# Last feed-forward of a decoder layer: chunks 6 to 17 of gate and up with tokens on the output's partitions

## The chip, the cores and the metric

The kernel runs on one core of a Trainium2 chip. The metric is device time of one execution in microseconds (us). The kernel before takes 858.42 us, the median of three runs (857.91 to 858.55).

## The reference

One layer, on 512 tokens of width 1024, all in float32: a feed-forward at half weight, a mixer (gated linear recurrence beside sliding-window attention), and a second feed-forward at half weight, each with a norm before and after.

```python
def swiglu(x, w_gu, w_down):
    gate, up = jnp.split(x @ w_gu, 2, axis=-1)
    return (jax.nn.silu(gate) * up) @ w_down

for l in range(DEPTH):                 # DEPTH = 1
    x = x + 0.5 * rms_norm(swiglu(rms_norm(x, ffn1_pre_g[l]), ffn1_w_gu[l], ffn1_w_down[l]), ffn1_post_g[l])
    y = hybrid_mixer(rms_norm(x, mix_pre_g[l]), ...)
    x = x + rms_norm(y, mix_post_g[l])
    x = x + 0.5 * rms_norm(swiglu(rms_norm(x, ffn2_pre_g[l]), ffn2_w_gu[l], ffn2_w_down[l]), ffn2_post_g[l])
```

The hidden width is 2816: 22 chunks of 128 for gate and as many for up.

## The kernel before

Every float32 product is made of three matrix multiplies on rounded parts: each operand is split into a high part (a cast on ACT, `whi_…` for weights, `hh…` for hidden values) and a low part (a subtraction on DVE, `wlo_…`, `hl…`), and high×high, high×low and low×high are added up in PSUM.

Gate and up of neighbouring chunks are the four blocks of a 2×2 block product, which is done with 7 block products instead of 8. It exists in two shapes.

- A **quad** (`Hidden.quad`, matmuls on L858) makes 2 chunks. Weights are stationary and 256 tokens move in each matmul; the output has hidden columns on its partitions. 168 matmuls.
- An **octo** (`Hidden.octo`, matmuls on L933) makes 4 chunks. Blocks of the input stay, and 512 weight columns move in each matmul; the output has tokens on its partitions. 168 matmuls as well. The down product wants hidden columns on the partitions, so the result is turned: DVE transposes 32×32 squares (L943), SP stores the 4 chunks to HBM in four transfers (`h_… <- z…`, L947), and they are fetched again (`hx… <- h_…`, L993 or L1006). The squares leave the tokens in a *dealt* order, 32 by 32 from the two halves, and the sums of the input blocks must be dealt too (L618 rather than L620).

The down product of 4 chunks also has two shapes: `seven_down`, 7 block products of the hidden values (84 matmuls of 512 columns, L1833 to L1835 in the last feed-forward), which needs sums of hidden blocks, each split into high and low; and a classical one, 24 matmuls of 512 columns for each chunk (L1809 to L1811). Results of a group are added into an array in HBM by accumulating transfers on POOL's queue (L1081).

The first feed-forward makes chunks 0 to 3 by plain products and chunks 4 to 19 by four octos, the second to fourth each followed by the `seven_down` of the group before it, so that an octo's hidden values have time for the way through HBM; chunks 20 and 21 come from a quad, beside which the fetched chunks 16 to 19 are split, and a classical down product of six chunks ends it. The last feed-forward (hidden tiles named `…b`) goes by `GROUPS2`, (0,6), (6,10), (10,14), (14,18), (18,22): chunks 0 to 5 by plain products and a classical down product; each of the next three groups by two quads and a `seven_down`; the last group by two quads and a last product, token block by token block (`ybl`, L1809 to L1811 again), followed by the norm, the residual (L1901 to L1921) and the output.

Weights come in units, handled by `Weights`, one list in the order of use. SP loads raw tiles (5 buffers); `take` hands out one unit and prepares those up to four ahead: for some units a combination of two blocks on DVE (`pre`, lines L292, `raw <- raw, raw`), the cast on ACT (L281), the subtraction on DVE (L285). `W.later(n, …)` defers work until n more units have been taken; `beside` hooks run between block products. Nothing else sets the order: each engine runs its instructions in the order in which the program lists them.

In the last group the hidden values of a quad come out in two halves, `u2` and `g1`: the first half of the tokens and the second. They are split on L871 (ACT) and L874 (DVE).

Of the kernel before, what the change touches and what calls it, by code (L numbers as in the profile page):

```python
# [8 lines left out]
F32 = mybir.dt.float32  # L9
# [8 lines left out]
NB = T // P  # L18
# [15 lines left out]
SEVEN_DOWN1, SEVEN_DOWN2 = (4, 16), (6, 18)  # L34
# [15 lines left out]
class Weights:  # L50
# [13 lines left out]
    def unit(self, raw, cast, low, pre=None):  # L64

        self.units.append((raw, cast, low, pre))
        self.left[raw] += 1
# [10 lines left out]
    def round(self):  # L78
        if self.rounded < len(self.units):
            raw, cast, _, pre = self.units[self.rounded]  # L80
# [39 lines left out]
def tile_layer(ctx: ExitStack, tc: tile.TileContext, out: bass.AP, **ins: bass.AP):  # L120
# [144 lines left out]
    def add_octo(w_gu, f, name):  # L265
# [12 lines left out]
        def unit(block, n, pre=None):  # L278
# [8 lines left out]
            W.unit(block[0], cast, low, pre)  # L287
# [101 lines left out]
    for f0, f1 in GROUPS2:  # L389
        for f in range(f0, f1, 2):  # L390
            (add_gate_up if f < CLASSIC2 else add_quad)(w2, f, "b")
        if SEVEN_DOWN2[0] <= f0 < SEVEN_DOWN2[1]:
            add_seven_down(ins["ffn2_w_down"], f0, "b")
        elif f1 < FC:
            for dh in range(2):
                for f in range(f0, f1, 4):
                    add_down(f, min(4, f1 - f), dh)
        else:
            for f in range(f0, f1, 4):
                for dh in range(2):  # L400
                    add_down(f, min(4, f1 - f), dh)
# [161 lines left out]
    class Next:  # L563
# [37 lines left out]
        def sums(self, k):  # L601
# [174 lines left out]
    class Hidden:  # L776
# [68 lines left out]
        def quad(self, f, last, ahead, seven_down=False, beside=lambda i: None):  # L845
# [3 lines left out]
            hs = None if seven_down else [(t2k(f"hh{n}{j}", F32R), t2k(f"hl{n}{j}", F32R)) for j in range(2)]  # L849
# [31 lines left out]
            u2, g1 = ((t2k if seven_down else wt)(f"{s}{n}") for s in ("u2", "g1"))  # L881
            seven(A, "b11", True)
            act.copy(B, A)
            seven(D, "t3", True)
# [18 lines left out]
            act.activation(g1, A, AF.Silu)  # L903
            if last:
# [1045 lines left out]
```

## Time and profile before

| what | value |
|---|---|
| median of three runs | 858.42 us |
| the profiled execution | 857.46 us, of which the span from first to last instruction 855.8 us |
| PE (matmuls) | 846.8 us, 99% of the span, 5252 instructions |
| DVE | 712.2 us, 83% |
| ACT | 520.3 us, 61% |
| POOL | 210.8 us, 25% |
| granted TensorE clock | 0.999 |

Times are microseconds from the start of the span. PE is TensorE, DVE VectorE, ACT ScalarE, POOL GpSimd, SP SyncE, whose queue starts most transfers. A busy engine need not be the one that sets the end; for that one reads what an engine waited for, and the chain of work that ended last. Rows of a group read: line, engine, operation, output<-inputs, count, duration. In stages by window, each engine has its busy time and, in brackets, its instructions; PEclk is the granted clock and the DMA share is the mean over 16 DMA engines. The durations that matmul rows show overlap each other; what one matmul costs is a run's length over its count.

### The profile page before, as it was taken

To read this page: it belongs to the slowest core of one execution; us is meant where nothing else is said; L and a number is where in the kernel's file an instruction comes from. 1 tells how busy PE (TensorE), PEld (TensorE's weight loads), DVE (VectorE), ACT (ScalarE), POOL (GpSimd) and SP (SyncE) were. 2 spreads that over 40 slices of the span, in tenths; PEclk is the share of its full clock that TensorE was granted. 3 is DMA by queue.
4 is the path that set the end of the run, shared out by engine and by line. 5 is a ranking of instruction groups with operands and counts; after the bars stand their busy time and mean duration, and the time that the engine had idled before them with its cause. 6 is when DMAs were issued, how large, how long until landed. Compare 5 with 4: busy or idle time off the path is not lost.

```text
span 855.8 us, 13837 instructions
## 1 busy us (share of the span) xinstructions
PE 846.8 (99%) x5252; PEld 762.6 (89%) x5252; DVE 712.2 (83%) x1008; ACT 520.3 (61%) x871; POOL 210.8 (25%) x228
## 2 busy tenths in 40 slices
PE   9999999999999999999999999999999999999996
PEld 9988788988988999988888899888998998998995
DVE  5988999979889865989888589788788789888856
ACT  6645746666575754648788346444566657658552
POOL 2022000230320424426453155211101303204402
PEclk9999999999999999999999999999999999999999
DMA  7249329397694999133301230356833946938912
GB/s 248 75 149 341 127 64 324 83 253 235 149 262 144 195 281 311 51 99 97 101 2 50 68 130 1 86 161 215 277 100 107 228 134 154 216 99 199 292 52 98
DMA packets 118914, 133.85 MB, mean 156 GB/s; under 512 B 23152, under 2 KB 85952, under 8 KB 118336
## 3 DMA queue, kind: packets, MB, share of 16 engines
q1 hardware_dynamic: 103504, 98.23, 36.2%
q0 software_dynamic: 15200, 34.61, 18.1%
q8 instruction: 41, 0.67, 0.3%
q14 instruction: 25, 0.20, 0.1%
q10 hardware_dynamic: 144, 0.13, 0.0%
HBM read 96.25 MB, written 36.70 MB: 155 GB/s over the span
## 4 chain that ended last, share of the span: by engine, by line
PE 87%; DVE 6%; ACT 3%; POOL 1%; DMA 1%; issue 1%; SPq 0%; DVEq 0%; ACTq 0%; POOLq 0%
PE ab L858 11%; PE aa L933 10%; PE db L858 5%; PE da L933 4%; PE yaa L1309 3%; PE bb L858 3%; PE ba L933 3%; PE yda L1309 2%; PE aa L858 1%; PE yb L1811 1%; PE yb L1810 1%; PE yb L1809 1%; PE wo L1764 1%; PE yea L1309 1%; PE yba L1309 1%
## 5 line engine op out<-in xcount | busy, mean ns | idle before, releaser
L1081 POOL DMA_DIRECT2D yp_a<-stage x42 | 36.4, 1084 | 179.8 <-ACT stage L1078 169.8
L1081 POOL DMA_DIRECT2D yp_b<-stage x42 | 36.8, 1139 | 148.3 <-ACT stage L1078 143.2
L479 PE MATMUL ya<-hha,whi_ad 128*128 128x512 f32 x62 | 24.1, 389 | 0.0
L481 PE MATMUL ya<-hha,wlo_ad 128*128 128x512 f32 x62 | 24.1, 389 | 0.0
L480 PE MATMUL ya<-hla,whi_ad 128*128 128x512 f32 x62 | 24.1, 389 | 0.0
L665 POOL TENSOR_TENSOR acca_r<-acca_r,sq_r 128x512 f32<-128x512 f32 x6 | 8.0, 1328 | 45.4 <-ACT sq_r L510 45.4
L1809 PE MATMUL yb<-whi_bd,hhb 128*128 128x512 f32 x48 | 18.7, 389 | 0.0
L1810 PE MATMUL yb<-wlo_bd,hhb 128*128 128x512 f32 x48 | 18.7, 389 | 0.0
L1811 PE MATMUL yb<-whi_bd,hlb 128*128 128x512 f32 x48 | 18.7, 389 | 0.0
L211 DVE TENSOR_TENSOR wlo_bd<-raw_bd,whi_bd 128x1024 fp32r<-128x1024 f32 x10 | 12.1, 1214 | 5.3 <-ACT whi_bd L206 5.3
L498 PE MATMUL an<-xh_mx,whi_xl 128*128 128x256 f32 x64 | 15.8, 287 | 0.0
L792 POOL TENSOR_TENSOR usb<-usb,gsb 128x512 f32<-128x512 f32 x5 | 7.2, 1443 | 34.1 <-DVE usb L789 22.8
L499 PE MATMUL an<-xh_mx,wlo_xl 128*128 128x256 f32 x64 | 15.5, 283 | 0.0
L1909 POOL TENSOR_TENSOR yp_b<-yp_b,grow 128x512 f32<-128x512 f32 x6 | 7.7, 1291 | 27.2 <-ACT ysq L1902 27.2
L479 PE MATMUL gt<-xh_mx,whi_gt 128*128 128x512 f32 x32 | 14.2, 444 | 0.0
L480 PEld LDWEIGHTS ya<-hla,whi_ad 128*128 128x128 f32 x62 | 11.6, 188 | 2.4
L479 PEld LDWEIGHTS ya<-hha,whi_ad 128*128 128x128 f32 x62 | 11.6, 188 | 2.4
L481 PEld LDWEIGHTS ya<-hha,wlo_ad 128*128 128x128 f32 x62 | 11.6, 188 | 2.4
L1810 PE MATMUL ybl<-wlo_bd,hhb 128*128 128x512 f32 (+1 forms) x36 | 13.2, 366 | 0.0
L1809 PE MATMUL ybl<-whi_bd,hhb 128*128 128x512 f32 (+1 forms) x36 | 13.2, 366 | 0.0
L1811 PE MATMUL ybl<-whi_bd,hlb 128*128 128x512 f32 (+1 forms) x36 | 13.2, 365 | 0.0
L1857 POOL DMA_DIRECT2D yp_b<-stage x8 | 4.4, 550 | 35.4 <-ACT stage L1856 35.0
(2157 smaller groups left out, 3723.5 us busy)
## 6 DMA issues: line engine op xcount, KB each, us to landing
yp_a<-stage POOLq DMA_DIRECT2D x50, 256.0 KB, 8.9
yp_b<-stage POOLq DMA_DIRECT2D x50, 256.0 KB, 7.5
h_a<-za SPq DMA_DIRECT2D x16, 256.0 KB, 4.2
hxa<-h_a SPq DMA_DIRECT2D x16, 256.0 KB, 18.4
raw_bd<-in_ffn_w_down SPq DMA_DIRECT2D x4, 1024.0 KB, 5.8
xn<-in_x SPq DMA_DIRECT2D x8, 256.0 KB, 4.2
xT_hbm<-xT POOLq DMA_DIRECT2D x2, 1024.0 KB, 9.4
yp_a<-yp_a SPq DMA_DIRECT2D x8, 256.0 KB
```

The costliest lines, as they stand in the source:

```text
L479: pe.matmul(ps, hi[:, k, :], xh, start=start, stop=False)
L480: pe.matmul(ps, hi[:, k, :], xl, start=False, stop=False)
L481: pe.matmul(ps, lo[:, k, :], xh, start=False, stop=stop)
L498: pe.matmul(ps[:, sl], hi[:, k, :], xh, start=k == 0, stop=False)
L499: pe.matmul(ps[:, sl], lo[:, k, :], xh, start=False, stop=False)
L858: pe.matmul(o, w[:, k, js], x, start=first and i + j + k == 0, stop=k == 3 and i == 2, skip_group_check=True)
L933: pe.matmul(b[tb], x[:, blk], w[:, k, :], start=first and q + k + j == 0, stop=q + k == 2 and j == 2, skip_group_check=True)
L1081: pool.dma_start(o, st.rearrange("p (a b) -> p a b", a=2) if len(o.shape) == 3 else st, accum_op=ALU.add)
L1309: pe.matmul(o, a[:, k, ms], x[:, js], start=first and i + k + m % 2 == 0, stop=k == 1 and i == 2, skip_group_check=True)
L1809: pe.matmul(ps, hh[:, blk], hi[:, k, cs], start=start, stop=False)
L1810: pe.matmul(ps, hh[:, blk], lo[:, k, cs], start=False, stop=False)
L1811: pe.matmul(ps, hl_[:, blk], hi[:, k, cs], start=False, stop=stop)
```

## The change

- Chunks 6 to 9, 10 to 13 and 14 to 17 of the last feed-forward are made by one octo each instead of two quads. Their hidden values go through HBM.
- The order becomes: octo(6), octo(10), `seven_down`(6), octo(14), `seven_down`(10), quad(18), the down product of chunks 14 to 17, quad(20), the last product. The down product of chunks 14 to 17 is classical; its four chunks are fetched into free tiles and split beside quad(18).
- The input sums of the last feed-forward are dealt, for the quads as well. So a block of 128 tokens of chunks 18 to 21 has columns from both `u2` and `g1`.
- In octo units, of the first feed-forward too, `fill` issues the combination and the cast of the next unit before the subtraction of the current one (`first`).
- In `seven_forms_of`, again for both feed-forwards, the hidden values that came back are split one half or one whole block product earlier: the first at 2.5 rather than 3.5, the second at 3.5 rather than 4.5, the third at 4.5 rather than 5.
- Some tiles are taken from other places (`spare`, `room`, `tiles`), and the load that was deferred to the first quad is now issued inside the classical down product of chunks 0 to 5.

```diff
@@ -88,7 +88,9 @@
         while self.split < min(self.taken + n, len(self.units)):
             if self.rounded == self.split:
                 self.round()
-            raw, _, low, _ = self.units[self.split]
+            if early and self.rounded == self.split + 1 < len(self.units) and self.units[self.rounded][4]:
+                self.round()
+            raw, _, low, _, _ = self.units[self.split]
             low(self.tiles[raw], *self.ready[self.split])
             self.split += 1
             self.left[raw] -= 1
@@ -284,7 +286,7 @@
             def low(raw, hi, lo):
                 dve.tensor_sub(lo, of(block), hi.bitcast(F32))
 
-            W.unit(block[0], cast, low, pre)
+            W.unit(block[0], cast, low, pre, True)
@@ -386,19 +388,23 @@
         for i in range(0, n, 2):
             add_unit(r, lambda raw, i=i: raw[:, i:i + 2, :], 2, T, f"bd{f + i}{dh}")
 
-    for f0, f1 in GROUPS2:
-        for f in range(f0, f1, 2):
-            (add_gate_up if f < CLASSIC2 else add_quad)(w2, f, "b")
-        if SEVEN_DOWN2[0] <= f0 < SEVEN_DOWN2[1]:
-            add_seven_down(ins["ffn2_w_down"], f0, "b")
-        elif f1 < FC:
+    for g, (f0, f1) in enumerate(GROUPS2):
+        if g == 0:
+            for f in range(f0, f1, 2):
+                (add_gate_up if f < CLASSIC2 else add_quad)(w2, f, "b")
             for dh in range(2):
                 for f in range(f0, f1, 4):
                     add_down(f, min(4, f1 - f), dh)
-        else:
-            for f in range(f0, f1, 4):
-                for dh in range(2):
-                    add_down(f, min(4, f1 - f), dh)
+            continue
+        (add_octo if f1 < FC else add_quad)(w2, f0, "b")
+        if f1 == FC:
+            for dh in range(2):
+                add_down(GROUPS2[g - 1][0], 4, dh)
+        elif g > 1:
+            add_seven_down(ins["ffn2_w_down"], GROUPS2[g - 1][0], "b")
+    add_quad(w2, f0 + 2, "b")
+    for dh in range(2):
+        add_down(f0, f1 - f0, dh)
@@ -603,11 +609,8 @@
 
             n = f"{self.name}{k}"
             xa, xb, t13, t24 = (wt(f"{s}_{n}") for s in ("xa", "xb", "ta", "tb"))
-            some = (lambda nm, dt: spare.pop() if spare else t2k(nm, dt)) if self.name != "a" else t2k
-            if self.name != "a" and k < 2:
-                spare.extend(fours(f"sums{k}", F32R))
-            b11 = some(f"b11_{n}", F32R)
-            highs = [some(f"{s}h_{n}", F32R) for s in ("b2", "t13", "t24")]
+            b11 = t2k(f"b11_{n}", F32R)
@@ -793,7 +796,7 @@
 
         def split(self, f):
             us, n = self.u.pop(f), f"{self.name}{f}"
-            hh, hl = t2k(f"hh{n}", F32R), t2k(f"hl{n}", F32R)
+            hh, hl = (spare.pop(), spare.pop()) if spare else (t2k(f"hh{n}", F32R), t2k(f"hl{n}", F32R))
             act.copy(hh, us)
             dve.tensor_sub(hl, us, hh.bitcast(F32))
             self.hs[f] = (hh, hl)
 
             def low_parts(x, h):
-                if seven_down:
-                    (self.seven_right if h else self.seven_left)(f, x, last)
-                    return
                 def own(t):
                     return dealt(t)[:, 2 * h:2 * h + 2] if self.nxt.dealt else t[:, HALF[h]]
@@ -996,13 +997,14 @@
                 self.forms, self.blocks = {}, {}
                 self.seven_left(f, x[0, 0], 0)
 
-            return {1: [fetch], 3.5: [begin], 4.5: [lambda: self.seven_right(f, x[0, 1], 0)], 5: [lambda: self.seven_left(f, x[1, 0], 1)],
-                    5.5: [lambda: self.seven_right(f, x[1, 1], 1)], 6: [lambda: self.steps.pop(0)()]}
-
-        def fetched(self, f, h_hbm):
+            first, second = ([lambda: self.seven_right(f, x[0, 1], 0)], [lambda: self.seven_left(f, x[1, 0], 1)]), [lambda: self.seven_right(f, x[1, 1], 1)]
+            step = [lambda: self.steps.pop(0)()]
+            return {1: [fetch], 2.5: [begin], 3.5: first[0], 4.5: first[1], 5.5: second, 6: step}
@@ -1797,7 +1786,7 @@
             W.fill(3)
     late = [(c, W.take(0)) for c in range(EARLY, KD)]
 
-    n2 = Next("f2", "ffn2_pre_g")
+    n2 = Next("f2", "ffn2_pre_g", dealt=True)
@@ -1834,34 +1823,57 @@
                 pe.matmul(banks[i], hh[:, js], lo[:, k, :], start=False, stop=False, skip_group_check=True)
                 pe.matmul(banks[i], hl_[:, js], hi[:, k, :], start=False, stop=k == 1, skip_group_check=True)
 
-    for g, (f0, f1) in enumerate(GROUPS2[:-1]):
-        if g:
-            if g == 1:
-                W.later(4, W.load, 2)
-            seven_down(hid, f0, by_tokens, lambda half, dh, i: parts[2 * half + i, dh])
-            continue
-        turns = [(turn_back, c) for c in range(KD)]
-        hs = hid.classic(f1, banks, {2.5: turns[:2], 3: turns[2:4], 3.5: [(n2.sums, 0)], 4: [(n2.lows, 0)] + turns[4:6], 4.5: [(n2.sums, 1)], 5: [(n2.lows, 1)] + turns[6:]}, AHEAD - 1)
+    def classic_down(hs, f0, f1, others=lambda dh, f: None, **kw):
         for dh in range(2):
-            ybanks = [bank(f"yb{g}{dh}{tb}") for tb in range(NB)]
                 if f % 2 == 0:
                     w = W.take()
                 for tb in range(NB):
                     mm3_out(ybanks[tb], hs[f - f0], tb, w, f % 2, ALL, f == f0, f == f1 - 1)
-                if g == 0 and (dh, f) in ((0, 0), (0, 2), (1, 2), (1, 4)):
-                    (n2.sums if f == 2 * dh else n2.lows)(2 + dh)
+                others(dh, f)
             for tb in range(NB):
                 st = t2k("stage")
                 act.activation(st, ybanks[tb], AF.Copy, scale=-1.0 if dh else 1.0)
-                pool.dma_start(parts[tb, dh], st)
-    f0, f1 = GROUPS2[-1]
+                pool.dma_start(parts[tb, dh], st, **kw)
+
+    h_hbm, room = {}, [r_tile] + 3 * [acc_tile]
+    down = lambda half, dh, i: parts[2 * half + i, dh]
+    for g, (f0, f1) in enumerate(GROUPS2):
+        if f1 == FC:
+            hid.fetched(before, h_hbm[before], lambda name: room.pop()(name))
+            todo = list(range(before, f0))
+            for i in range(2):
+                spare.extend(fours(f"hs{i + 2}", F32R))
+            hid.quad(f0, False, AHEAD, beside=lambda i: hid.split(todo.pop(0)) if 1 < i < 6 else None)
+            classic_down([hid.hs.pop(f) for f in range(before, f0)], before, f0, accum_op=ALU.add)
+            continue
+        if g:
+            h_hbm[f0] = hid.octo(f0, hid.seven_forms_of(before, h_hbm[before]) if g > 1 else {})
+            if g > 1:
+                seven_down(hid, before, by_tokens, down, hid.forms, AHEAD - 1)
+            before = f0
+            continue
+        for i in range(2):
+            spare.extend(fours(f"hs{i}", F32R))
+        turns = [(turn_back, c) for c in range(KD)]
+        hs = hid.classic(f1, banks, {2.5: turns[:2], 3: turns[2:4], 3.5: [(n2.sums, 0)], 4: [(n2.lows, 0)] + turns[4:6], 4.5: [(n2.sums, 1)], 5: [(n2.lows, 1)] + turns[6:]}, AHEAD - 1)
+
+        def others(dh, f):
+            if (dh, f) in ((0, 0), (0, 2), (1, 2), (1, 4)):
+                (n2.sums if f == 2 * dh else n2.lows)(2 + dh)
+            if (dh, f) == (1, 2):
+                W.load(2)
+
+        classic_down(hs, f0, f1, others)
     in_hbm, parts = parts, {}
+    tiles = [r_tile("yp_r")] + [acc_tile(f"yp_a{i}") for i in range(3)] + fours("yp", F32)
     for tb in range(NB):
         for dh in range(2):
-            parts[tb, dh] = t2k(f"yp_b{tb}{dh}")
+            parts[tb, dh] = tiles.pop()
             pool.dma_start(parts[tb, dh], in_hbm[tb, dh])
-    hs = hid.chunks(f0, f1, ahead=5)
+    hid.quad(f0 + 2, True, 5)
+    hs = [hid.hs.pop(f) for f in range(f0, f1)]
     x_rows = []
     for i in range(2):
         x = wpool.tile([P, 2 * D], F32, tag="raw", name=f"x_rows{i}", bufs=NRAW)
```

The new order on the engines, at three places. First DVE at the first octo of the program (first feed-forward); `raw … <- raw …` is a combination, `wlo … <- raw …, whi …` the subtraction that needs ACT's cast `whi`. Before:

```order
L285 TENSOR_TENSOR wlo_ap__931<-raw_ax__875,whi_ap__930 128x1024
L292 TENSOR_TENSOR raw_ax__785<-raw_ax__785 128x2x512
L285 TENSOR_TENSOR wlo_aq__959<-raw_ax__785,whi_aq__958 128x1024
L292 TENSOR_TENSOR raw_ax__875<-raw_ax__875 128x2x512
L285 TENSOR_TENSOR wlo_aq__980<-raw_ax__875,whi_aq__979 128x1024
L292 TENSOR_TENSOR raw_ax__785<-raw_ay__920,raw_ax__785 128x2x512
L285 TENSOR_TENSOR wlo_ar__1001<-raw_ax__785,whi_ar__1000 128x1024
```

and with the change:

```order
L294 TENSOR_TENSOR raw_ax__785<-raw_ax__785 128x2x512
L287 TENSOR_TENSOR wlo_ap__930<-raw_ax__878,whi_ap__929 128x1024
L294 TENSOR_TENSOR raw_ax__878<-raw_ax__878 128x2x512
L287 TENSOR_TENSOR wlo_aq__958<-raw_ax__785,whi_aq__957 128x1024
L294 TENSOR_TENSOR raw_ax__785<-raw_ay__920,raw_ax__785 128x2x512
L287 TENSOR_TENSOR wlo_aq__979<-raw_ax__878,whi_aq__978 128x1024
L294 TENSOR_TENSOR raw_ax__878<-raw_ay__923,raw_ax__878 128x2x512
```

Each combination now stands one subtraction earlier. Before, `raw_ax__785` was combined, cast, and subtracted with nothing between; now a subtraction of another unit lies between a combination and the subtraction that needs its cast.

Second, ACT in octo(10), where the hidden values of chunks 6 to 9 (`hxb`), fetched by SP, are split for the `seven_down` that follows; `u2` is the copy of the PSUM tile `ab`, which PE writes again two block products later. With the change (before, no such row stands in the last feed-forward):

```order
L283 CAST whi_bt__6896<-raw_bx__6624 128x1024
L283 CAST whi_bu__6915<-raw_by__6677 128x1024
L807 CAST hha_6934<-hxb_6871 128x512
L939 COPY u2b_6806<-ab_6794 128x512
L939 COPY u2b_6807<-ab_6795 128x512
L283 CAST whi_bu__6940<-raw_by__6698 128x1024
```

The first split of fetched values stands ahead of the copy of PSUM, with nothing else between them.

Third, ACT at the end of the last quad (chunks 20 and 21; `hhb` is the high part of their hidden values, one tile for each chunk). Before:

```order
L871 CAST hhb_8694<-u2b_8704 128x256
L871 CAST hhb_8696<-u2b_8704 128x256
L903 ACTIVATE g1b_8705<-ab_8698 128x512
L871 CAST hhb_8694<-g1b_8705 128x256
L871 CAST hhb_8696<-g1b_8705 128x256
```

and with the change:

```order
L871 CAST hhb_8216<-u2b_8226 128x2x4x32
L871 CAST hhb_8218<-u2b_8226 128x2x4x32
L904 ACTIVATE g1b_8227<-ab_8220 128x512
L871 CAST hhb_8216<-g1b_8227 128x2x4x32
L871 CAST hhb_8218<-g1b_8227 128x2x4x32
```

The instructions are the same; each now writes pieces of 32 tokens into every block of 128, where before the first two wrote token blocks 0 and 1 and the last two blocks 2 and 3.

More of the change, by code (lines that the diff above doesn't have):

```diff
@@ L62, in raw, with unit @@
         return len(self.raws) - 1
-    def unit(self, raw, cast, low, pre=None):
-        self.units.append((raw, cast, low, pre))
+    def unit(self, raw, cast, low, pre=None, first=False):
+        self.units.append((raw, cast, low, pre, first))
         self.left[raw] += 1
@@ L79, in round @@
         if self.rounded < len(self.units):
-            raw, cast, _, pre = self.units[self.rounded]
+            raw, cast, _, pre, _ = self.units[self.rounded]
             if pre:
@@ L605, in sums @@
             xa, xb, t13, t24 = (wt(f"{s}_{n}") for s in ("xa", "xb", "ta", "tb"))
[L606 to L610 removed]
+            b11 = t2k(f"b11_{n}", F32R)
+            highs = [t2k(f"{s}h_{n}", F32R) for s in ("b2", "t13", "t24")]
             l, r = HALF
@@ L843, in seven_right, with quad @@
             self.steps = [lambda: self.low("s2"), last_sum, lambda: self.low("s4"), lambda: self.low("a22"), lambda: self.low("s1")]
-        def quad(self, f, last, ahead, seven_down=False, beside=lambda i: None):
+        def quad(self, f, last, ahead, beside=lambda i: None):
             n = f"{self.name}{f}"
             l, r = HALF
-            hs = None if seven_down else [(t2k(f"hh{n}{j}", F32R), t2k(f"hl{n}{j}", F32R)) for j in range(2)]
+            hs = [(t2k(f"hh{n}{j}", F32R), t2k(f"hl{n}{j}", F32R)) for j in range(2)]
             def seven(b, form, first, ahead=AHEAD):
@@ L880, in quad @@
             p1, p7, u4 = (wt(f"{s}{n}") for s in ("p1", "p7", "u4"))
-            u2, g1 = ((t2k if seven_down else wt)(f"{s}{n}") for s in ("u2", "g1"))
+            u2, g1 = (wt(f"{s}{n}") for s in ("u2", "g1"))
             seven(A, "b11", True)
             act.copy(B, A)
+            beside(0)
             seven(D, "t3", True)
@@ L903, in quad @@
             act.activation(g1, A, AF.Silu)
+            beside(6)
             if last:
@@ L909, in quad @@
                 W.later(2, low_parts, g1, 1)
-            if not seven_down:
-                for j in range(2):
-                    self.hs[f + j] = hs[j]
+            for j in range(2):
+                self.hs[f + j] = hs[j]
         def octo(self, f, beside):
@@ L1041, in classic @@
             return [self.hs.pop(f) for f in range(n)]
-        def chunks(self, f0, f1, ahead=AHEAD):
-            for f in range(f0, f1, 2):
-                self.quad(f, f == f1 - 2, ahead if f == f1 - 2 else AHEAD)
-            return [self.hs.pop(f) for f in range(f0, f1)]
         def last_chunks(self, f, h_hbm, extra):
@@ L1051, in last_chunks, with seven_down @@
             todo = list(range(f, f + 4))
-            self.quad(f + 4, True, AHEAD, beside=lambda i: (extra.get(i, lambda: None)(), self.split(todo.pop(0)) if i > 1 else None))
+            self.quad(f + 4, True, AHEAD, beside=lambda i: (extra.get(i, lambda: None)(), self.split(todo.pop(0)) if 1 < i < 6 else None))
             return [self.hs.pop(c) for c in range(f, f + 6)]
-        def seven_forms(self, f):
-            self.forms, self.blocks = {}, {}
-            for i in (0, 1):
-                self.quad(f + 2 * i, i, AHEAD, True)
-            return self.forms
-    def seven_down(hid, f, one, part, forms=None, ahead=AHEAD):
-        free = [] if forms is None else [r_tile] + 3 * [acc_tile]
-        forms = forms or hid.seven_forms(f)
+    def seven_down(hid, f, one, part, forms, ahead):
+        free = [r_tile] + 3 * [acc_tile]
         A, B, Dd, E_ = ([bank(f"y{s}{hid.name}{f}{i}") for i in range(2)] for s in "abde")
```

5 lines of the change are left out of this document (3 added, 2 removed).

## The prediction

> **What bounds the kernel now.** I read the page first: the busy shares, the row of slices, the chain that ended last.
>
> ```profile
> PE 846.8 (99%) x5252; PEld 762.6 (89%) x5252; DVE 712.2 (83%) x1008; ACT 520.3 (61%) x871; POOL 210.8 (25%) x228
> PE   9999999999999999999999999999999999999996
> PE 87%; DVE 6%; ACT 3%; POOL 1%; DMA 1%; issue 1%; SPq 0%; DVEq 0%; ACTq 0%; POOLq 0%
> ```
>
> PE is busy in every slice but the last, so no stage hides behind another engine. Next the waits of PE, all that the view lists:
>
> ```profile
> PE warm L1155 <- POOL ident masks.py:199: 1.4, 1, 1.4
> PE aa L933 <- ACT ba L938: 0.6, 1, 0.6
> ```
>
> One is at the very start, one in the first octo. So the kernel is a stream of matmuls, and a change of the stream's length shows in full, as long as the other engines still keep ahead of it. The windows by stage tell by how much they do:
>
> ```profile
> core 0: us, PE busy (x) PEld busy (x) DVE busy (x) ACT busy (x) POOL busy (x), PEclk, DMA share, GB/s
> 78.30:117.30 39.00, 38.38 (x170) 31.44 (x169) 34.78 (x49) 23.66 (x31) 2.06 (x3) 1.00 0.49 168
> 117.30:155.40 38.10, 38.10 (x170) 31.55 (x169) 35.75 (x40) 25.15 (x35) 0.00 (x0) 1.00 0.57 194
> 175.50:213.60 38.10, 38.10 (x170) 31.56 (x169) 33.71 (x36) 27.11 (x37) 5.54 (x7) 1.00 0.90 245
> 213.60:233.80 20.20, 20.20 (x170) 20.18 (x169) 18.58 (x22) 11.08 (x17) 6.74 (x8) 1.00 0.59 140
> 575.80:608.40 32.60, 32.60 (x145) 27.03 (x144) 28.84 (x41) 17.84 (x26) 2.97 (x6) 1.00 0.66 210
> 608.40:648.80 40.40, 40.40 (x338) 40.36 (x338) 32.10 (x34) 22.51 (x30) 1.40 (x3) 1.00 0.44 146
> 648.80:667.80 19.00, 19.00 (x86) 15.73 (x85) 16.93 (x19) 14.25 (x22) 6.67 (x8) 1.00 0.70 170
> 826.90:855.80 28.90, 22.10 (x110) 18.60 (x108) 16.93 (x35) 9.95 (x27) 7.75 (x6) 0.96 0.19 73
> ```
>
> Rows 1 to 3 are octos of the first feed-forward, row 4 a `seven_down` there; then the classical down product of chunks 0 to 5 in the last feed-forward, a pair of quads, its `seven_down`, and the last product with the tail. Octo and quad pair do the same 4 chunks.
>
> **The matmul stream.** What a matmul costs is the length of a run in the chain of waits over its count:
>
> ```profile
> 122.88 5.44 PE da L933 x24
> 611.48 2.88 PE db L858 x24
> ```
>
> 512 columns: 5.44/24 = 226.7 ns. 256 columns: 2.88/24 = 120.0 ns. Twice 120.0 is 240.0, so halving a matmul adds 13.3 ns. The change takes away 3 pairs of quads (6 x 168 = 1008 matmuls of 256 columns, -120.96 us), adds 3 octos (3 x 168 = 504 of 512), drops one `seven_down` (84 of 512) and adds a classical down product of four chunks (4 x 24 = 96 of 512): 516 more of 512, +116.98 us. Together **-3.98 us**; by stages, -6.7 for the octos and +2.7 for the down product. The granted clock is 1.00 in octo and quad rows alike, so neither shape is slowed by it.
>
> The Trainium skill has a rule that speaks against this step: "TensorE: Matmul & The Clock Gate", section "Back-to-back issue gap", gives N / 2.4 + 2.5 ns for an isolated matmul at full clock. By it a matmul of 256 would take 109.2 ns and one of 512 215.8, and the step would be an estimated -110.0 + 111.4 = +1.3 us. Both figures lie under the rows above, and the fixed part that they imply, 2.5 ns, is not the 13.3 of the rows; I go by the rows.
>
> **The first octo's stall.** The octo in row 1 took 39.00 us, of which PE was busy for 38.38; the next took 38.10. The extra is 0.9 us. Its cause, DVE and ACT in that place:
>
> ```profile
> 79.19 1.22 DVE L292 TENSOR_TENSOR raw_ax__875<-raw_ax__875 128x1024 f32<-128x1024 f32 x1
> 81.52 1.23 DVE L285 TENSOR_TENSOR wlo_aq__980<-raw_ax__875,whi_aq__979 128x1024 fp32r<-128x1024 f32 x1 [1.12 <-ACT whi_aq__979 L281]
> 82.67 1.22 DVE L292 TENSOR_TENSOR raw_ax__785<-raw_ay__920,raw_ax__785 128x1024 f32<-128x1024 f32 x1
> 89.39 0.49 ACT ba L938
> 89.93 5.75 PE aa L933 x24
> ```
>
> Combination, cast and subtraction of one unit run one after the other, 82.67 - 79.19 = 3.48 us for each unit, and DVE idles 1.12 of it for the cast. ACT meets the copy `ba`, for which PE waits, only behind this. With `first` the next combination stands ahead of the subtraction, so it fills the idle time: about 1.1 us less for each of the last four units, more than the 0.6 that PE waits. I take **-0.9 us**; bounds 0 (something else is late instead) and -0.9.
>
> **The end of the last quad.** With dealt tokens, token block 0 of the last product needs columns from `g1`, which come last:
>
> ```profile
> 827.10 0.60 ACT L903 ACTIVATE g1b<-ab 128x512 f32<-128x512 f32 x1 [0.72 <-PE ab L858]
> 828.45 0.71 ACT L871 CAST hhb<-g1b 128x256 fp32r<-128x256 f32 x2 [0.76 <-DVE g1b L877]
> 828.89 0.76 DVE L874 TENSOR_TENSOR hlb<-g1b,hhb 128x256 fp32r<-128x256 f32 x2 [0.47 <-ACT hhb L871]
> 828.28 0.39 PE L1809 MATMUL ybl<-whi_bd,hhb 128*128 128x512 f32 x1
> ```
>
> The last row is the first matmul on chunk 20: the last product starts at 826.90 and chunks 18 and 19 occupy 6 matmuls. The high part of chunk 20, the first of the two casts, is there at about 828.45 + 0.36 = 828.8, so PE waits 0.5 to 0.6; its low part comes at 828.89 + 0.38 = 829.3, when PE, thus delayed, wants it. **+0.6 us**; bounds 0.5 and 0.9 (the whole cast pair). Writing in pieces of 32 costs nothing more: the first feed-forward's quad already writes so (`hha`), the last one's not yet:
>
> ```profile
> L871 ACT CAST hha<-u2a x2: 402/402/403, 315.0 to 315.3; 128x256 fp32r<-128x256 f32 x2
> L871 ACT CAST hhb<-u2b x4: 400/404/408, 805.6 to 826.0; 128x256 fp32r<-128x256 f32 x4
> ```
>
> **What I cost at nothing, and its cover.** Dealt sums are 8 instructions for a pair of input blocks in place of 2:
>
> ```profile
> L618 DVE SCALAR_TENSOR_TENSOR xa_a<-xT,g,R_a x16: 342/345/347, 30.5 to 68.5; 128x128 f32<-128x128 f32 x16
> L620 DVE SCALAR_TENSOR_TENSOR xa_f<-xT,cols,R_f x4: 734/746/748, 555.4 to 601.9; 128x512 f32<-128x512 f32 x4
> ```
>
> 8 x 0.345 = 2.8 us against at least 1.5: at most 1.3 us more for each of four, two of them inside 575.80 to 608.40, where DVE is idle for 32.6 - 28.8 = 3.8. In the octos DVE does 33.7 + 18.6 = 52.3 us for an octo and a `seven_down` (rows 3 and 4). In the last feed-forward the two last 38.1 + 19.0 = 57.1, a load of 92%; in the first 58.3, 90%, without a wait of PE. PE would wait only where DVE had over 57.1 - 52.3 = 4.8 us more to do in such a period. The earlier splits of fetched values move DVE and ACT work by a block product or less inside the same octos, and ACT there is busy for 27.1 of 38.1. The splits of chunks 14 to 17 beside quad(18) are what the first feed-forward's last quad does, also without a wait of PE; uncovered they would cost 4 x 0.62 = 2.5 us (the cast's row `L797` below). The accumulating transfers of chunks 14 to 17 come late on POOL, and the loads of the sum are queued behind them:
>
> ```profile
> 790.76 4.41 POOL L1081 DMA_DIRECT2D yp_b<-stage  x5 [1.19 <-ACT bb L883]
> 803.45 1.08 POOL L1863 DMA_DIRECT2D yp_b<-yp_b  x2 [0.30 <-DMA yp_b<-stage]
> 831.38 1.28 POOL L1909 TENSOR_TENSOR yp_b<-yp_b,grow 128x512 f32<-128x512 f32 x1 [20.00 <-ACT ysq L1902]
> ```
>
> In the changed order that down product ends one quad (20.2) ahead of the last product, its last stores are issued some 4 us later, and as here their sums stand 803.45 - 795.17 = 8.3 us after that, at about 814. The first value is wanted some 3 us into the last product (POOL's multiplication of it, at 831.38, starts 4.5 in), so at least 8 us remain for the loads. Nothing is lost unless those 8 go.
>
> **The sum.** -3.98 - 0.9 + 0.6 = -4.3 us on the profiled execution: span 855.8 to 851.5, its time 857.46 to 853.2. The median of the runs shown is 0.96 above the profiled one; 858.42 - 4.3 = **854.1 us**. Own range: 852.8 (no wait at the end, a little noise) to 855.6 (the first stall stays, the last wait is 0.9).
>
> **Rivals.** *DVE falls behind in the octos.* At 92% a late unit is made up slowly. For it speaks that octo(6) opens with units whose weights SP loads under the end of the classical product, as the first octo of row 1 did; against it that octos 2 and 3 ran at 38.10 with the tighter old order. If each of three octos loses what the first one did, 3 x 0.9 = 2.8 us: 856.9, between 855.6 and 858.5 for one or more such chains.
>
> *The way through HBM is late* (the slower side). SP's fetches, and the first casts of what they brought:
>
> ```profile
> hxa<-h_a SPq DMA_DIRECT2D x16, 256.0 KB, 18.4
> 129.93 3.43 SPq L993 DMA_DIRECT2D hxa<-h_a  x4
> 137.29 0.62 ACT L804 CAST hha<-hxa 128x512 fp32r<-128x512 f32 x1
> L1006 SPq DMA_DIRECT2D hxa<-h_a x4: 333/354/404, 296.8 to 298.7; - x4
> L797 ACT CAST hha<-hxa x4: 620/622/622, 301.5 to 308.6; 128x512 fp32r<-128x512 f32 x4
> ```
>
> In the second octo (it starts at 117.28) the fetch is issued 12.65 in. In the changed order ACT has the first cast of the fetched block ahead of the copy `u2`, and PE overwrites what `u2` copies in the fifth block product, 4 x 5.44 = 21.8 us in. The mechanism decides where a fetch lands later than 21.8 - 12.65 = 9.1 us after its issue. At the 18.4 of the page octo(10) loses 9.3 us, and quad(18), whose fetch has even less time, some 8: 871. Against it: the cast at 137.29 follows 7.4 us after the issue and did not wait, and at 301.5 it came 4.7 after. The 18.4 belongs to a fetch that nobody wanted earlier. I keep it for one of the two places as well, 862 to 871.
>
> *Matmuls are priced by their columns alone*: the 13.3 ns are no fixed part but belong to what a quad does otherwise. Then 1008 x 256 columns go and 516 x 512 come, 6144 more at 226.7/512 ns, +2.7 us: 858.42 + 2.7 + 0.6 - 0.9 = 860.8. Against it stand the two rows themselves, in streams without a wait. (The skill's rule is a milder form of it: 859.4.)
>
> *The sum in HBM is late at the tail*: those 8 us go, and up to 4 more: 854 to 858.
>
> **How the numbers follow.** The forecast gets 0.72; DVE behind in the octos 0.17; the way through HBM 0.06; pricing by columns 0.02; a late tail 0.03. A measurement tells about 0.2% from no change, 1.7 us: faster is under 856.7, slower over 860.1. Faster: 0.72, half of DVE's case, and part of the tail's, **0.80**. Same: the other half and the rest of the tail, **0.11**. Slower: the way through HBM, pricing by columns, and a remainder, **0.09**. The range 852.8 to 857.6 holds the forecast and some two thirds of DVE's case: 0.8.
>
> **What would show it.** In the changed profile: three octos of 38.1 us; the first octo of the program at 38.1 too, and no wait of PE for `ba`; a wait of PE for `hhb` of 0.5 to 0.6 near the start of the last product; a classical down product of 21.8; the last product starting at 826.9 - 4.9 = 822.0. Wrong would be: octos of 39 and more, with PE waiting for ACT or DVE; PE waiting behind a cast of `hxb`; matmuls in the octos off 226.7 ns.

## The result and the profile after

The changed kernel takes 854.15 us, the median of four runs (854.09 to 854.25); the kernel before, on the same chip, 858.48 (857.91 to 858.84). The ratio is 0.9950, with a 95% interval from 0.9933 to 0.9968: 4.3 us faster, where 854.1 was predicted. The profiled executions differ by less: 854.25 against 857.46, spans of 852.5 and 855.8.

From the page of the changed kernel, and all waits of PE that the view lists in it (PEld is the load of stationary blocks, which overlaps PE):

```profile
PE 843.3 (99%) x4760; PEld 738.7 (87%) x4760; DVE 708.6 (83%) x1030; ACT 514.9 (60%) x859; POOL 205.1 (24%) x222
```

```profile
PE warm L1144 <- POOL ident masks.py:199: 1.4, 1, 1.4
PE ybl L1798 <- ACT hhb L871: 0.5, 1, 0.5
PE xtp L1091 <- DMA xn<-in_x: 0.2, 1, 0.2
```

The wait for `ba` is gone, and the wait for `hhb` in the last product is new, both as forecast. The third is at the start of the program, where PE waits for the input `x`; a second profile of the same kernel (below) doesn't have it. The stages of the changed kernel (columns as before): the first octo of the program; octo(6), octo(10), `seven_down`(6), octo(14), `seven_down`(10), quad(18), the classical down product, quad(20), the last product and the tail.

```profile
78.80:116.90 38.10, 38.10 (x170) 31.54 (x168) 33.98 (x48) 23.57 (x30) 1.52 (x3) 1.00 0.49 172
607.90:645.90 38.00, 38.00 (x169) 31.50 (x168) 28.12 (x28) 19.61 (x25) 1.31 (x3) 1.00 0.31 112
646.00:684.00 38.00, 38.00 (x169) 31.49 (x168) 36.94 (x41) 25.48 (x34) 0.00 (x0) 1.00 0.57 194
684.00:703.00 19.00, 19.00 (x85) 15.75 (x84) 18.46 (x22) 13.11 (x20) 7.03 (x8) 1.00 0.62 148
703.10:741.10 38.00, 38.00 (x169) 31.50 (x168) 33.78 (x36) 25.48 (x34) 5.27 (x6) 1.00 0.91 244
741.20:760.20 19.00, 19.00 (x86) 15.73 (x85) 16.71 (x21) 10.50 (x16) 5.24 (x6) 1.00 0.62 145
760.20:780.70 20.50, 20.37 (x169) 20.17 (x168) 15.91 (x18) 16.72 (x26) 6.99 (x8) 1.00 1.11 249
780.70:802.50 21.80, 21.80 (x99) 18.05 (x97) 13.78 (x15) 9.19 (x15) 4.47 (x6) 1.00 0.73 196
802.50:822.60 20.10, 20.10 (x169) 20.10 (x168) 9.41 (x10) 10.08 (x15) 9.10 (x15) 1.00 0.96 288
822.70:852.50 29.80, 22.37 (x109) 18.41 (x108) 16.90 (x35) 10.06 (x27) 7.75 (x6) 0.96 0.19 71
```

All four octos take 38.1 and PE never pauses in them. Two small losses remain. Quad(18) takes 20.5 where half a pair takes 20.2; in the chain that ended last, its third block product starts only after ACT's copy `bb`. PE's list above doesn't have this wait, because the view gives it to the load of the stationary block (PEld, 0.3). The chain, and PE's matmuls in that place:

```profile
764.73 0.95 ACT whi_bu__7827 L248
765.67 0.50 ACT bb L883
766.22 3.14 PE ab L861 x24
...
765.81 0.28 PE L861 MATMUL db<-t13h_f,wlo_bq__7708 128*128 128x256 f32 x1
766.22 0.38 PE L861 MATMUL ab<-t24h_f,whi_br__7732 128*128 128x256 f32 x1
766.44 0.28 PE L861 MATMUL ab<-t24l_f,whi_br__7732 128*128 128x256 f32 x1
```

From 765.81 to 766.44 are 0.63 us for two matmuls of 0.120, a loss of 0.39. And the last product with its tail takes 29.8 where it took 28.9; PE at chunk 20:

```profile
823.81 0.39 PE L1800 MATMUL ybl<-whi_bd,hlb 128*128 128x512 f32 x1
824.66 0.50 PE L1798 MATMUL ybl<-whi_bd,hhb 128*128 128x512 f32 x1 [0.46 <-ACT hhb L871]
825.00 0.40 PE L1799 MATMUL ybl<-wlo_bd,hhb 128*128 128x512 f32 x1
```

From 823.81 to 825.00 are 1.19 us for two matmuls of 0.227, a loss of 0.74. Octo(10) and the `seven_down` behind it leave DVE little room: 36.94 + 18.46 = 55.4 of 57.1 us.

Where PE stands at two marks tells how the 3.3 us of the two spans come about. First in the profile before, then in the changed one, the last matmul ahead of the first octo, the first octo, and in the changed one the start of the last product:

```profile
78.04 0.39 PE L481 MATMUL ya<-hha,wlo_ad 128*128 128x512 f32 x1
78.27 0.62 PE L933 MATMUL aa<-whi_ap__878,b_a 128*128 128x512 f32 x2
```

```profile
78.59 0.39 PE L487 MATMUL ya<-hha,wlo_ad 128*128 128x512 f32 x1
78.82 0.39 PE L934 MATMUL aa<-whi_ap__874,b_a 128*128 128x512 f32 x1
...
822.65 0.40 PE L1798 MATMUL ybl<-whi_bd,hhb 128*128 128x512 f32 x1
```

The changed kernel reached its first octo 0.55 us later. It started the last product 826.90 - 822.65 = 4.25 us earlier all the same, 4.8 us gained in between (0.9 in the first octo, the rest below), and took some 1.0 us longer from there to the end. Without the late start the spans would differ by about 3.8.

### The profile page after: what moved, and what is told of

It is laid out like the page before. It is cut to its first block, busy times and chain, and to the rows that moved or that the text cites. A ratio compares the mean times of both kernels' runs of the same rounds, so it can differ in the third digit from the quotient of the medians.

```text
span 852.5 us, 12903 instructions
## 1 busy us (share of the span) xinstructions
PE 843.3 (99%) x4760; PEld 738.7 (87%) x4760; DVE 708.6 (83%) x1030; ACT 514.9 (60%) x859; POOL 205.1 (24%) x222
## 4 chain that ended last, share of the span: by engine, by line
PE 91%; DVE 4%; ACT 1%; issue 1%; POOL 1%; DMA 1%; SPq 0%; DVEq 0%; ACTq 0%
PE aa L934 10%; PE ab L934 7%; PE da L934 5%; PE db L934 3%; PE yaa L1298 3%; PE ba L934 3%; PE ab L861 2%; PE yb L1800 2%; PE yb L1798 2%; PE yb L1799 2%; PE yda L1298 2%; PE bb L934 2%; PE ya L485 2%; PE ya L486 2%; PE ya L487 2%
## 5 line engine op out<-in xcount | busy, mean ns | idle before, releaser
L1070 POOL DMA_DIRECT2D yp_b<-stage x28 | 24.5, 1033 | 139.1 <-ACT stage L1067 125.7
L1838 POOL DMA_DIRECT2D yp_b<-stage x16 | 11.4, 897 | 59.9 <-ACT stage L1837 59.5
L1798 PE MATMUL yb<-whi_bd,hs 128*128 128x512 f32 x64 | 24.9, 390 | 0.0
L1799 PE MATMUL yb<-wlo_bd,hs 128*128 128x512 f32 x64 | 24.9, 390 | 0.0
L1800 PE MATMUL yb<-whi_bd,hs 128*128 128x512 f32 x64 | 24.9, 389 | 0.0
L213 DVE TENSOR_TENSOR wlo_bd<-raw_bd,whi_bd 128x1024 fp32r<-128x1024 f32 x14 | 16.9, 1216 | 6.3 <-ACT whi_bd L208 6.3
L208 ACT CAST whi_bd<-raw_bd 128x1024 fp32r<-128x1024 f32 x14 | 14.6, 1050 | 3.9 <-DMA raw_bd<-in_ffn_w_down 2.4
L1800 PEld LDWEIGHTS yb<-whi_bd,hs 128*128 128x128 f32 x64 | 12.0, 188 | 2.5
L1799 PEld LDWEIGHTS yb<-wlo_bd,hs 128*128 128x128 f32 x64 | 12.0, 188 | 2.5
L1798 PEld LDWEIGHTS yb<-whi_bd,hs 128*128 128x128 f32 x64 | 12.0, 188 | 2.4
L1798 PE MATMUL ybl<-whi_bd,hhb 128*128 128x512 f32 (+1 forms) x36 | 13.3, 370 | 0.5 <-ACT hhb L871 0.5
```

What stands on the lines that cost most here:

```text
L213: low.tensor_sub(two(lo, x), x, two(hi.bitcast(F32), x))
L1070: pool.dma_start(o, st.rearrange("p (a b) -> p a b", a=2) if len(o.shape) == 3 else st, accum_op=ALU.add)
L1798: pe.matmul(ps, hh[:, blk], hi[:, k, cs], start=start, stop=False)
L1799: pe.matmul(ps, hh[:, blk], lo[:, k, cs], start=False, stop=False)
L1800: pe.matmul(ps, hl_[:, blk], hi[:, k, cs], start=False, stop=stop)
```

## The experiments

The kernel before was timed beside every set of kernels; since they ran on several chips, ratios to it are compared, and 1% is 8.6 us.

**The start.** The kernel before, a second time.

> The kernel before once more, for a second profile. The two profiles differ at the start: the first octo begins at 78.27 us in the one before and at 78.82 in the changed one, where PE waits for the transfers of x. Theory: the start varies from execution to execution by about half a microsecond to one, and the profile before had an early one; then this span lies between 856 and 857.2, the first octo is again 39.0, and nothing after it differs. Rival: a wait inside the octos or quads varies; then the octo start is at 78.3 again and a later stage is longer.

Measured: span 856.1, first octo again at 78.27, and again PE waits 0.6 in it for `ba`. So the start does not explain this one; the 0.3 us more came later, with a wait of PE of 0.3 in the mixer's attention. The theory's place was wrong; the rival's form holds, though not in octo or quad. In later profiles of the changed kernel and its variants the first octo began at 78.3 to 78.9. So the start does vary by half a microsecond (the changed kernel alone gave 78.82 and 78.32), but that is one of several small spreads, and why the kernel before spreads over 857.3 to 860.2 in 27 runs and the changed one over 853.9 to 854.5 is left open.

**The order of combination and subtraction alone**, in the kernel before (`first` for octo units, nothing else):

```diff
+            if early and self.rounded == self.split + 1 < len(self.units) and self.units[self.rounded][4]:
+                self.round()
```

> The kernel before with the new order of combination and subtraction in octo units alone. Theory: the first octo goes from 39.00 to 38.08 and the 0.1 to 0.2 lost in the first feed-forward's quad may go too: 0.9 to 1.1 us less, 857.4 to 857.6, PE waits no more for ba. Rival: the wait only moves to another octo or to the quad, no change, 858.5.

Measured: ratio 0.9989 (0.9979 to 0.9998), 857.33 against 857.96. PE waits no longer for `ba`; span 854.9 against 856.1 for the kernel before on this chip. The theory's 0.9 lies within the interval, the rival's no change just outside; the 0.2 us in the first feed-forward's quad stayed.

**The changed kernel without it:**

```diff
-            W.unit(block[0], cast, low, pre, True)
+            W.unit(block[0], cast, low, pre)
```

> The changed kernel with the old order in octo units. Theory: only the first octo of the program stalls, 0.9 us more: 855.1. Rival (DVE behind): the three new octos of the last feed-forward, where DVE has 57.1 us for an octo and a seven_down instead of 58.3, stall as well, 0.9 each or more: 856.0 to 857.8.

Measured: ratio 0.9992 (0.9984 to 1.0001), 857.58: 0.0042 above the changed kernel's 0.9950, 3.6 us, almost the whole gain. The loss has the size that the rival gives, but not its place. PE's waits in this kernel (leaving out the one at the start of the program), and its octo(14), `seven_down`(10) and quad(18):

```profile
PE ab L861 <- ACT bb L883: 0.7, 1, 0.7
PE aa L934 <- ACT ba L939: 0.5, 1, 0.5
PE ybl L1798 <- ACT hhb L871: 0.5, 1, 0.5
PE yab L1822 <- ACT stage L1067: 0.3, 1, 0.3
PE yeb L1824 <- DVE hls L814: 0.2, 1, 0.2
...
703.50:741.90 38.40, 38.40 (x169) 31.45 (x169) 34.12 (x37) 26.47 (x37) 6.79 (x8) 1.00 0.94 249
741.90:762.10 20.20, 19.71 (x86) 15.62 (x85) 18.20 (x21) 9.96 (x15) 5.24 (x6) 1.00 0.56 132
762.10:783.10 21.00, 20.35 (x169) 20.14 (x168) 16.13 (x18) 17.24 (x27) 6.96 (x8) 1.00 1.11 244
```

Only the second wait is in the first feed-forward, where the first octo takes 0.8 us more again. Octo(6) and octo(10) run at 38.1 as in the changed kernel. Octo(14) loses 0.3, `seven_down`(10) 1.1 (20.2 where 19.0 is usual), and quad(18) 0.5 more than in the changed kernel. Together these are 2.7 of the 3.6 us; this profile is 0.9 faster than the median of its kernel, and where the slower runs lose the rest isn't shown. DVE at the start of octo(14), in this kernel and then in the changed one:

```profile
707.21 1.22 DVE L294 TENSOR_TENSOR raw_bx__6979<-raw_by__7145,raw_bx__6979 128x1024 f32<-128x1024 f32 x1
709.60 1.23 DVE L287 TENSOR_TENSOR wlo_br__7279<-raw_bx__6979,whi_br__7278 128x1024 fp32r<-128x1024 f32 x1 [1.17 <-ACT whi_br__7278 L283]
710.74 1.22 DVE L294 TENSOR_TENSOR raw_bx__7000<-raw_by__7180,raw_bx__7000 128x1024 f32<-128x1024 f32 x1
713.12 1.22 DVE L287 TENSOR_TENSOR wlo_br__7322<-raw_bx__7000,whi_br__7321 128x1024 fp32r<-128x1024 f32 x1 [1.17 <-ACT whi_br__7321 L283]
715.40 1.22 DVE L287 TENSOR_TENSOR wlo_bs__7339<-raw_by__7145,whi_bs__7338 128x1024 fp32r<-128x1024 f32 x1
```

```profile
707.85 1.22 DVE L287 TENSOR_TENSOR wlo_br__7321<-raw_bx__7000,whi_br__7320 128x1024 fp32r<-128x1024 f32 x1
708.98 1.22 DVE L294 TENSOR_TENSOR raw_bx__7000<-raw_bx__7000 128x1024 f32<-128x1024 f32 x1
710.12 1.22 DVE L287 TENSOR_TENSOR wlo_bs__7338<-raw_by__7145,whi_bs__7337 128x1024 fp32r<-128x1024 f32 x1
712.51 1.22 DVE L287 TENSOR_TENSOR wlo_bs__7357<-raw_by__7183,whi_bs__7356 128x1024 fp32r<-128x1024 f32 x1
```

The old order takes 713.12 - 709.60 = 3.5 us for a unit, 1.17 of it idle; the new one 2.3 to 2.4. At 713 the old order is at the second `br`, which the new one did at 708 (the octos start at 703.5 and 703.1). From the start of octo(10) to this place DVE sat idle five times for 1.2 us until ACT had cast a block, four of them around the start of octo(14), 5.9 us in all; in the changed kernel not once. That DVE came late into `seven_down`(10) and quad(18) by this is read from the order of the waits: there PE waited for copies of ACT and a low part of DVE. DVE's busy share hid this chain through ACT.

**What a matmul costs.** Octos of the last feed-forward with each 512-column matmul issued as two of 256; then as one of 384 and one of 128:

```diff
-pe.matmul(b[tb], x[:, blk], w[:, k, :], ...)
+for cs in HALF if self.name == "b" else (ALL,):
+    pe.matmul(b[tb][:, cs], x[:, blk], w[:, k, cs], ...)
```

(Both kernels compute wrong values, presumably because the second piece starts the sum in its bank anew; no run shows that. The columns multiplied are the same.)

> The changed kernel with each 512-column matmul of the last feed-forward's octos issued as two of 256, the same columns with the same stationary block: 504 more matmuls. Theory (a matmul has a fixed part of 13.3 ns): 504 x 13.3 = 6.7 us more, 860.9, octos of 40.3. Rival (priced by columns): no change, 854.2, and the octos' gain over quads would come from something else. By the Trainium skill's rule (TensorE: Matmul & The Clock Gate, Back-to-back issue gap) the fixed part is 2.5 ns: 1.3 us more, 855.4.

> The changed kernel with each 512-column matmul of the last feed-forward's octos issued as one of 384 and one of 128. Halving cost 6.3 us, 12.4 ns for each added matmul. If a matmul has a fixed part of 13.3 ns and 0.417 ns a column whatever its width: again 504 x 13.3 = 6.7 us more, 860.8. If a matmul can't go faster than its stationary block is loaded, 120 ns as in the quads, the one of 384 takes 173 and the one of 128 120: 504 x 66.6 = 33.6 us more, 887.7.

Measured: halves 860.33, ratio 1.0026 (1.0017 to 1.0035), 0.0076 above the changed kernel: 6.5 us, the 6.7 of the theory. 384 and 128: 884.93 in its one run, 30.9 above 854.05. The stage of octo(6) in each:

```profile
607.60:647.90 40.30, 40.30 (x337) 40.30 (x336) 28.60 (x29) 19.59 (x25) 1.35 (x3) 1.00 0.31 106
```

```profile
607.60:655.60 48.00, 48.00 (x336) 48.00 (x335) 29.79 (x30) 19.61 (x26) 1.31 (x3) 1.00 0.27 89
```

Halved octos take what quads take, 40.3. The same number of matmuls, cut unevenly, takes 48.0: 48.0/168 = 285.7 ns for the two, near the 173 + 120 = 293 of the second expectation (the load sets the pace) and far from the 240 of the first. So "13.3 ns a matmul" is no law below 256 columns. The column after PE, for the loads of the stationary block (PEld), is full in both, but that tells little: a load is shown with 0.19 us and overlaps the next. When the loads start tells more, first in the halved octos and then in the uneven ones:

```profile
619.94 0.31 PEld L935 LDWEIGHTS ab<-whi_br__6463,t24l_f 128*128 128x128 f32 x2
620.18 0.31 PEld L935 LDWEIGHTS ab<-wlo_br__6464,t24h_f 128*128 128x128 f32 x2
```

```profile
620.06 0.30 PEld L935 LDWEIGHTS db<-wlo_bq__6405,t13h_f 128*128 128x128 f32 x2
620.35 0.30 PEld L935 LDWEIGHTS db<-whi_bq__6404,t13h_f 128*128 128x128 f32 x2
```

In the halved octo(6) they are 0.12 us apart, all alike. In the uneven one the second of a pair starts 0.30 - 0.19 = 0.11 after the first, and the next pair 0.18 later: 107 to 109 ns and 177 to 180 in turn. No load of it follows another by less than 107 ns, although every second matmul has only 128 columns. That the load limits this matmul fits these starts; no run varies the load alone. The Trainium skill, "TensorE: Matmul & The Clock Gate", section "LDWEIGHTS (loading the stationary operand)", gives P / 1.2 ns for a load of P columns, for 128 an estimated 106.7 ns; the 107 to 109 agree with it. Its section "Back-to-back issue gap" says that in a stream of loads and matmuls the spacing is set by both, which fits as well. The 2.5 ns that the same section adds for an isolated matmul would make halving cost an estimated 1.3 us; the 6.5 us measured don't fit it. A quad's 120.0 ns lie above the closest loads, so the load's spacing alone doesn't explain them, and what the 13.3 ns consist of stays open.

**The changed kernel again, and its two losses.** The last product with chunks 18 and 19 for both output halves first, in its first token block:

```diff
-steps = [(i, f) for fs in (range(f0, f0 + 4), range(f0 + 4, f1)) for i in range(2) for f in fs]
+steps = [(i, f) for fs in (range(f0, f0 + 2), range(f0 + 2, f1)) for i in range(2) for f in fs]
```

(with the weight units in that order), and quad units with `first`:

> The changed kernel once more, beside its variants on one chip. Theory: 854.1 to 854.3 as before, with the same two losses in its profile: 0.39 us in quad(18), where PE waits for the copy bb, and 0.74 at the first matmul on chunk 20 of the last product. Rival: one of them varies from execution to execution, as the stalls of the kernel without the new order did.

> The changed kernel, but the first token block of the last product uses chunks 18 and 19 for both output halves (12 matmuls) before chunks 20 and 21; the weight units follow that order. Theory: PE reaches chunk 20 6 x 0.227 = 1.36 us later, the high part is there, the wait of 0.74 is gone: 853.4. Rival: the first value of the block is complete later and the tail keeps the time, or the weights of the new second unit are late: 854.2.

> The changed kernel with the new order of combination and subtraction in quad units as well. Theory: before quad(18) DVE sat idle twice for a cast (0.57 and 1.17 us) and ACT twice for a combination (2.13 and 1.64), so the copy bb came 0.4 late on ACT; with the idle time filled it comes a microsecond earlier and the 0.39 is gone: 853.8. Rival: the copy bb is late behind the copies of the seven_down's results, not behind casts, then nothing changes: 854.2.

> Both of these edits in the changed kernel. Theory: the two losses are at different places and add up, 0.39 + 0.74 = 1.1 us less: 853.0 to 853.1. Rival: the sum is smaller than its parts because the tail takes some back.

Measured on one chip: the changed kernel 854.05 (853.91 to 854.45), with the same two losses in its profile; the reordered last product 853.68 (853.48 to 853.85); quad units with `first` 855.43 (854.87 to 855.71), and both 854.51 (853.93 to 855.60), where 853.8 and 853.0 to 853.1 were expected. In the profile of the reordered one no wait for `hhb` is left and the stage from the start of the last product to the end is 0.8 shorter. The gain between the medians is 0.4, not 0.74. In the profiles the first octo of the reordered one began 0.5 later, at 78.85, than in the changed kernel's beside it, at 78.32; whether the medians differ by the start as well isn't shown.

The other two fell short. A unit's combination overwrites a block in place; in a quad the combination of `r` overwrites what the subtraction of `q` has yet to read, so those two kernels compute wrong values. An octo has two units of each kind, one for each half of the input rows, and a unit of the other half stands between. In quad(18) the wait went, but the first feed-forward's quad now waits:

```profile
PE aa L861 <- ACT ba L883: 1.2, 1, 1.2
```

**A version without either loss.** The reordered last product, and the new order in the last feed-forward's quads only for units `q` and `s`, which overwrite nothing that is still read:

```diff
+            W.unit(block[0], cast, low, pre, name == "b" and n in "qs")
```

> The changed kernel with the reordered last product and, in the last feed-forward's quads, the combination of units q and s ahead of the subtraction before them (these two overwrite nothing that the subtraction still reads; r and t would). Theory: the copy bb in quad(18) was 0.4 late because DVE and ACT took turns on units p to r; one turn less of 1.1 us and the 0.39 is gone, on top of the reordered last product: 853.3, PE without a wait in quad(18) and at hhb. Rival: the 0.39 comes from the copies of the seven_down's results on ACT: 853.7.

Measured: 853.28 us (852.76 to 853.31), ratio 0.9935 (0.9921 to 0.9948), where 853.3 was expected. The listed waits of PE are three, and none is in the last feed-forward. The two edits are in one kernel, but they act in different places; that the second one removes the loss in quad(18) shows in its length, which is a quad's usual one again:

```profile
760.40:780.60 20.20, 20.20 (x170) 20.18 (x169) 14.35 (x17) 15.78 (x25) 6.81 (x8) 1.00 1.11 248
```

**The place of the splits.** The changed kernel with the old places:

```diff
-return {1: [fetch], 2.5: [begin], 3.5: first[0], 4.5: first[1], 5.5: second, 6: step}
+return {1: [fetch], 3.5: [begin], 4.5: first[0], 5: first[1], 5.5: second, 6: step}
```

> The changed kernel with the split of the fetched values at the old places, half a block product to a whole one later. Theory as predicted: the place costs nothing, 854.1. Rival: what is split later falls together with the seven_down's casts; then PE waits in the seven_down for a low part (hls or hla), 0.3 to 2 us more.

Measured: 855.83, ratio 0.9969 (0.9957 to 0.9981), 0.0019 above the changed kernel: 1.6 us. The intervals of the two ratios overlap, but all five runs (855.48 to 856.40) lie above all eight of the changed kernel (853.91 to 854.45), beside kernels before whose medians agree to 0.2. The rival holds in its direction and size, not in its place: PE waits in `seven_down`(10) for the copy of a result (`stage`, 0.2), in quad(18) longer for `bb` (0.6), and in the first feed-forward's down product for `hha` (0.2). With the slower matmuls next to each wait these places lose 0.5, 0.5 and 0.6 us; that they follow from ACT's splits standing later is read from the order, not shown by a run of its own.

**The way through HBM made late.**

```diff
+                if (self.name, f) == ("b", 6):
+                    sync.dma_start(hbm.tile([186, 2 * F], F32, name="other"), ins["ffn2_w_gu"][0, :186])
```

> The changed kernel with 4.2 MB more copied from HBM to HBM on SP's queue between the store of chunks 6 to 9 and their fetch (the copy is used by nothing). In the changed kernel the fetch lands 3.8 us after its issue at 657.64, and the copies of u2 end at 663.0, 4.7 us before PE overwrites what they read. Theory of the slower rival: at the 400 GB/s that the queue reaches here the fetch lands some 10 us later, 5 to 6 beyond the slack, and PE waits that long in octo(10) for u2: 859 to 860; the weights of the seven_down come later too and may add to it. Rival: the engines share the transfers, the fetch passes the copy and nothing is lost: 854.1.

Measured: 865.18 us in its one run, span 863.5, 11.0 above the changed kernel's 852.5. First the changed kernel's ACT in octo(10), then this one's, with its wait of PE and its stages:

```profile
661.42 0.62 ACT L807 CAST hha<-hxb 128x512 fp32r<-128x512 f32 x1 [0.81 <-DMA hxb<-h_b]
661.94 1.10 ACT L939 COPY u2b<-ab 128x512 f32<-128x512 f32 x2
```

```profile
674.46 0.62 ACT L807 CAST hha<-hxb 128x512 fp32r<-128x512 f32 x1 [13.87 <-DMA hxb<-h_b]
674.99 1.07 ACT L939 COPY u2b<-ab 128x512 f32<-128x512 f32 x2
...
PE ab L934 <- ACT u2b L939: 7.8, 1, 7.8
...
675.70:681.30 5.60, 5.60 (x13) 4.39 (x14) 4.82 (x7) 4.65 (x7) 0.00 (x0) 0.50 1.05 408
681.60:684.00 2.40, 2.40 (x12) 1.93 (x12) 2.40 (x3) 1.78 (x3) 0.00 (x0) 1.00 0.82 246
```

The first part of the fetch, issued at 657.32, landed 17.1 us later, 13.3 later than in the changed kernel where some 10 had been expected, and the time is 865 instead of 859 to 860. PE waited for `u2` as the theory says: 17.1 less the predicted margin of 9.1 is 8.0, and the wait is 7.8. On top, the granted clock was still 0.50 for 5.6 us after the wait; in them matmuls started 0.43 us apart instead of 0.227, which cost 2.9 us more with the first and the last of the stretch. Nobody had expected that. Wait and slow clock make up 10.8 of the 11.0. The fetch did not pass the transfer ahead of it on its queue.

## Why the prediction was right, and where not

- **The matmul stream.** Forecast -3.98. From the first octo of the last feed-forward to the last product's start, -3.66 with quad(18)'s 0.39 in it, so -4.05 without: right, and the price of halving was confirmed alone (6.5 of 6.7). The rival that prices matmuls by their columns alone is thereby refuted. That the price is a fixed part of each matmul, whatever its width, was not confirmed: below 256 columns it isn't.
- **The first octo.** Forecast -0.9, measured 39.0 to 38.1. Right, and a second 0.2 went in the first feed-forward's quad, which I had not counted.
- **What `first` is worth.** Here one step failed, though the sum did not show it. I priced `first` as the first octo's stall alone and took the new octos' cover from DVE's busy time: PE would wait only where DVE had over 4.8 us more to do, and octos 2 and 3 had run "at 38.10 with the tighter old order". Without it the changed kernel loses 3.6 us, because DVE's idle time for ACT's casts, 5.9 us up to 713, counts like work. So the rival "DVE falls behind in the octos", with 2.8 us, names the right engine and nearly the right size, and this part of the change is what prevents it; but octo(6) and octo(10) lose nothing, and most of the loss comes behind octo(14). The load of 92% that I took was that of a later octo of the first feed-forward; octo(10), the second of its row, has 97%.
- **Costed at nothing: the earlier splits.** The prediction let them neither cost nor gain. Moving them forward does not cost anything, but with the old places 1.6 us are lost, 1.0 of them in the last feed-forward: like `first`, the move is what lets the stream's -3.98 show in full.
- **The last product.** Forecast +0.6, bounds 0.5 and 0.9; measured 0.74 at chunk 20, and some 1.0 to the end of the span, of which 0.2 in the last stores. Right in cause and place, a little more than the bound of 0.9 in all.
- **Not foreseen:** quad(18), +0.39. It is DVE's and ACT's chain once more, at a quad, where the new order was not applied.
- **The sum.** -4.3 was forecast, about -3.8 measured in the two profiles at equal starts, and -4.3 between the medians. On the profiled execution the forecast was 853.2 and 854.25 came: 1.05 too little, half of it the late start and the rest quad(18) and the last product, less the 0.2 in the first feed-forward's quad. The median was hit to 0.05 because the forecast carried over the 0.96 by which the median of the kernel before lay above its profiled execution; in the changed kernel it lies 0.1 below. That is luck.
- **The way through HBM.** In the changed kernel the first part of the fetch landed 3.8 us after its issue and left 4.7 us; the rule for its price was right to 0.2 us before the clock's part.
- **The sum in HBM.** It was not late: the loads of it were issued by 812, and POOL's first multiplication, at 827.90, waited for ACT alone.

## What to carry to other kernels

Where PE is busy all the time, count matmuls by width and price each width from a run of that width; that carried the forecast of the stream. Then look for the chain that feeds it: an engine with idle time in its busy share may still be the one that is late, if combination, cast and subtraction alternate between two engines. Here the octos without the new order gave 0.7 us (ratio 0.9992, no change within its interval), the new order alone 0.9, and both together 4.3: a shorter stream pays only if the engines that feed it keep up, and their idle pieces count against them. Setting the next unit's first step ahead of the current unit's last may be done only where the step overwrites nothing that is still to be read.

## What the runs showed of the hardware

- A wait of PE of 7.8 us was followed by 5.6 us at a granted clock of 0.50, so it cost 10.8 in all. The clock was 1.00 for the first 3.3 us of the wait and 0.50 from 3.8 us on. Waits of up to 1.2 us were followed by one slower matmul only (about 0.1 us). The Trainium skill, "TensorE: Matmul & The Clock Gate", section "What's actually happening", says that the clock halves after at least one idle window of about 3.4 us and comes back after at least one such window of sustained work. The fall here agrees; the 5.6 us of work at half clock are more than one window and less than two.
- Of matmuls with a load of the stationary block each, two of 256 columns take 240 ns, one of 384 and one of 128 take 286; in octo(6) of the latter the closest loads start 107 ns apart.
- A transfer of 4.2 MB from HBM to HBM, issued ahead on the same queue, put off the landing of the first part of a 1 MB fetch from 3.8 to 17.1 us.
